# A one-core hybrid block: POOL's phase chain moved behind the last split, and the scaling of the inputs divided between DVE and ACT

## The chip, the cores and the metric

The kernel runs on one core of a Trainium2 chip. The metric is the device time of one execution in microseconds (us), taken as the median of several runs. Engines: PE (matrix multiply) with its weight loads PEld, DVE (elementwise), ACT (activations, copies), POOL (elementwise, and DMA issue), SP (DMA issue). SBUF is the memory on the chip that all of them read; PE writes its results to PSUM, which DVE and ACT read.

## The reference, cut to what matters

One layer of a block: a mixer out of an S5 state-space branch and a gated linear attention (HGRN), then a mixture of experts. The inputs are `x` (1024 tokens of 1024 features) and a context `ctx` (256 tokens), float32. The change concerns how the normalised, modulated inputs are made, and tables of the S5 branch.

```python
mod = jax.nn.silu(c) @ w_ada + b_ada              # shift sh1, scale sc1, ... for the tokens
mod_c = jax.nn.silu(c_ctx) @ w_ada + b_ada        # csh1, csc1, ... for the context
h  = rms_norm(x,   norm1_g) * (1.0 + sc1)  + sh1  # rms_norm: t * rsqrt(mean(t*t) + eps) * g
hc = rms_norm(ctx, norm1_g) * (1.0 + csc1) + csh1
z  = h @ w_in                                     # u (256, for S5), q, ff, fb, i, g_out, gates
zc = hc @ w_in
# S5: powers of exp(lam*dt) per state, products with b_bar and c; the scan over the tokens
```

The root (`rsqrt`) belongs to a token; the factor `norm1_g * (1 + sc1)` and the shift `sh1` belong to a feature.

## The kernel before

x and ctx are held transposed: features on the 128 partitions, 8 tiles k = 0 .. 7 of 128 features, tokens along the columns. There are three streams r: the 256 context tokens (r = 0), tokens 0 to 511 (r = 1), tokens 512 to 1023 (r = 2).

All large products are made in float32 parts: an operand is split into a high part (ACT rounds it to `F32R`) and a low part (DVE subtracts the high part), and `mm3` (lines 81 to 84) does high x high (L82), low x high (L83) and high x low (L84). So a matmul over tile k of a stream waits for ACT's high part `hH` or `hcH` and for DVE's low part.

The front of the kernel is a `manual_schedule` block: in it each engine works in the order in which the lines stand. Its steps:

- `s5_tables` makes tables of the S5 branch on DVE, in short instructions. Then POOL makes `phases(1, G)`: the powers 0 to 159 of a phase for 8 groups, by doubling, 8 rounds of 6 elementwise products and sums (`cmul_steps`, L1233 to L1248), of 8, 16, .. 512 and at last 248 columns, in the buffer `big1`, and two DMAs to `phd` (L1316). Then POOL makes `ca` (two halves of 6 products of 1152 columns), each followed by two DMAs to `cad` (L1328). The same phases for the other direction, `phases(0, V)` in `big0`, are on DVE, handed to the caller as a generator: the caller runs 24 steps of it at once, 3 later and the rest behind the last split. Its two DMAs are issued by POOL as well.
- `stats(r)`: ACT squares the tiles, PE sums them, `rsqrt` (L89 to L93: a root on ACT, a reciprocal and three short instructions on DVE, two of which read two SBUF operands) gives the root per token, and PE spreads it over all partitions into PSUM, `prs[r]` (L279).
- `mods(g)`: PE multiplies a quarter of `w_ada` by the activations of c. Quarters 2 and 3 give the factor `am` early; quarters 0 and 1 give the shift, which `shift` (L317) writes into `mod`.
- `scaled(r, k)` (L284, DVE): x tile times `am` (per partition) times `prs[r]` (PSUM). `split(r, k)`: ACT adds the shift and rounds to the high part (L292); DVE adds the shift again and subtracts the high part (L295).
- The loop over k splits streams 0 and 1, and `z_step` multiplies each tile for the first two 128-column blocks of `w_in` (the u of S5). Four tiles of stream 1 are scaled ahead of the loop and four inside it. Then `scaled(2, k)` and `split(2, k - 1)` run over stream 2, `z_half` does the second half of the tokens, and u goes as `us0`, `us1` to DRAM (`u_out`: `us0` by 8 DMAs of POOL, `us1` by 8 of SP).

Behind the block a planner orders each engine's work. `s5_tables2` makes `wts` on DVE (12 products of 1024 columns), PE transposes them, and matrices `kts` are put together in buffers of the same names `big0` and `big1` and sent to `kd`. `values(0)` multiplies all tokens by the i columns of `w_in`, ten tiles in three PSUM buffers "z", which ACT copies into `vc` (context) and `vt` (L429). Pool "up" with `us0` and `us1` is closed at the end of the block, and pool "vp" with `vt` and `vc` is opened at its place: `vt` begins at the first byte of `us0`, and `vc` lies within `us1`.

Of the kernel before, what the change touches and what calls it, by code (L numbers as in the profile page):

```python
# [10 lines left out]
F32 = mybir.dt.float32  # L11
# [3 lines left out]
AF = mybir.ActivationFunctionType  # L15
ALU = mybir.AluOpType
# [8 lines left out]
P = 128  # L25
D = 1024
KD = D // P
# [16 lines left out]
def tile_kernel(ctx: ExitStack, tc: tile.TileContext, A: dict, dbg=None):  # L44
    nc = tc.nc
    V, S, G, PE = nc.vector, nc.scalar, nc.gpsimd, nc.tensor
# [34 lines left out]
    def mm3(out, lh, ll, rh, rl, start, stop):  # L81
        PE.matmul(out, lh, rh, start=start, stop=False)  # L82
        PE.matmul(out, lh, rl, start=False, stop=False)  # L83
        return PE.matmul(out, ll, rh, start=False, stop=stop)  # L84
# [19 lines left out]
    def half(dt=F32):  # L104

        return hp.tile([P, 512], dt, name="xl", bufs=2 * KD)

    def ctx_row(dt=F32):
        return hcp.tile([P, LC], dt, name="xcl", bufs=KD + 1)
# [32 lines left out]
    am = frp.tile([P, KD, 2], F32, name="am")  # L142
# [9 lines left out]
    def z_half(H, L, n, out=None, ks=range(KD)):  # L152
        ps = zp.tile([P, 512], F32, name="z") if out is None else out
        for k in ks:
            ws = slice(k * P, k * P + P)
            ts = slice(n * 512, n * 512 + 512)
            lastmm[0] = mm3(ps, H[:, ws], L[:, ws], hH[:, k, ts], hL[n][k], k == 0, k == KD - 1)
        return ps
# [8 lines left out]
    with tc.manual_schedule(), tc.tile_pool(name="stp", bufs=1, space=PSUM) as qp, ExitStack() as small:  # L167
        q = small.enter_context(tc.tile_pool(name="st", bufs=1))
# [50 lines left out]
        def am_steps():  # L219
# [6 lines left out]
            )  # L226

        s5t = s5_tables(nc, tc, A, cad, phd, r8d, am_steps, *s5in)
        next(s5t)
        S.activation(lg, lg, AF.Exp)  # L230
# [10 lines left out]
        prs = [qp.tile([P, 512], F32, name=f"prs{r}") for r in range(3)]  # L241
# [38 lines left out]

        def scaled(r, k):
            rows_, _, lo, hi = streams[r]
            c = 1 if r == 0 else 0
            V.scalar_tensor_tensor(  # L284
                rows_[k], rows_[k], am[:, k, c : c + 1], prs[r][:, : hi - lo], ALU.mult, ALU.mult
            )

        def split(r, k):
            rows_, H, lo, hi = streams[r]
            c, ho = (1, 0) if r == 0 else (0, lo)  # L290
            xk, Hk, sh = rows_[k], H[:, k, ho : ho + hi - lo], mod[:, k, c : c + 1]
            S.activation(Hk, xk, AF.Identity, bias=sh)  # L292
            Lk = half(F32R) if r else ctx_row(F32R)
            (hL[r - 1] if r else hcL).append(Lk)
            return V.scalar_tensor_tensor(Lk, xk, sh, Hk.bitcast(F32), ALU.add, ALU.subtract).ins  # L295

        def some(g, n):
            for _ in range(n):
                next(g, None)
# [5 lines left out]
        def u_half(m, n, ps):  # L305
            for c in range(4):

                dst = us[m][:, :, 32:160].rearrange("p j (r c) -> p c j r", c=8)[:, n * 4 + c]
                V.tensor_copy(dst, ps.rearrange("p (c j r) -> p c j r", c=4, j=8)[:, c])

        def u_out(m, E):
            for j in range(8):
                E.dma_start(ud[m].rearrange("(j c) g k -> j g c k", j=8)[j], us[m][:, j])
            dump("us%d" % m, us[m])
# [7 lines left out]
        for g in (2, 3):  # L322
            some(md[g], 3)
        s5mid = next(s5t)
        some(s5mid[3], 24)
        some(st[0], KD + 1)
        some(st[1], 4)
        some(st[0], 1)
# [3 lines left out]
        for k in range(KD - 1):  # L332
            scaled(0, k)
        some(md[0], 1)
        some(st[1], 1)
        scaled(0, KD - 1)
        some(s5mid[3], 3)
        some(st[1], 1)
        some(md[0], 2)
        for k in range(4):  # L340
            scaled(1, k)
        shift(0)
        some(md[1], 2)
        split(0, 0)
        split(1, 0)
        some(md[1], 1)
        H0 = high_w(raws[0])
        L0 = low_w(raws[0], H0)
        split(0, 1)
        split(1, 1)  # L350
        shift(4)
# [7 lines left out]
        def z_step(m, k):  # L359
            H, L = ((H0, L0), (H1, L1))[m]  # L360
            zc_tile(H, L, (pc0, pc1)[m], [k])
            z_half(H, L, 0, (z00, z10)[m], [k])
# [2 lines left out]
        z_step(0, 1)  # L365
        z_step(1, 0)
        for k in range(2, KD):
            if k + 2 < KD:
                scaled(1, k + 2)
            split(0, k)  # L370
            split(1, k)
            some(st[2], PAT[k - 2])
            z_step(0, k)
            z_step(1, k - 1)
# [8 lines left out]
        for k in range(KD + 1):  # L383
            if k < KD:
                scaled(2, k)
            if k in (2, 5):
                u_half(k // 5, 0, (z00, z10)[k // 5])
            if k:
                lastL = split(2, k - 1)
        u_half(0, 1, z_half(H0, L0, 1))  # L390
        u_out(0, G)
        u_half(1, 1, z_half(H1, L1, 1))
# [6 lines left out]


    with tc.issue_after(lastL):
        some(s5mid[3], 99)
    if stop_after <= 1:
        ws_.close(); s5s.close(); early.close(); zs.close(); fr.close()
        return
# [424 lines left out]
    q = xs_.enter_context(tc.tile_pool(name="wo", bufs=1, reuse_waits="tile"))  # L830
# [261 lines left out]
def s5_tables(nc, tc, A, cad, phd, r8d, more, q, qt, par, bt, ct):  # L1092
    V, S, G, PE = nc.vector, nc.scalar, nc.gpsimd, nc.tensor
# [41 lines left out]
    def tsc(a, s1, op0, s2=None, op1=None, o=None):  # L1135
        o = t16() if o is None else o
        if op1 is None:
            E.tensor_scalar(o, a, s1, None, op0)
        else:
            E.tensor_scalar(o, a, s1, s2, op0, op1)  # L1140
        return o
# [11 lines left out]
    r = tsc(n, -PI_HI, ALU.mult)  # L1153
# [71 lines left out]
    def cmul_steps(or_, oi, ar_, ai, br, bi, shp, E=V, own=None):  # L1225

        n_ = int(np.prod(shp))
        t = temp(E, n_, own)
        if len(shp) == 2:
            t = t.rearrange("p (a b) -> p a b", a=shp[0])  # L1230
        if len(shp) == 3:
            t = t.rearrange("p (a b c) -> p a b c", a=shp[0], b=shp[1])
        E.tensor_tensor(or_, ar_, br, ALU.mult)  # L1233
        yield
        E.tensor_tensor(t, ai, bi, ALU.mult)
        yield
        E.tensor_tensor(or_, or_, t, ALU.subtract)
        yield
        E.tensor_tensor(oi, ar_, bi, ALU.mult)
        yield  # L1240
        t2 = temp(E, n_, own)
        if len(shp) == 2:
            t2 = t2.rearrange("p (a b) -> p a b", a=shp[0])
        if len(shp) == 3:
            t2 = t2.rearrange("p (a b c) -> p a b c", a=shp[0], b=shp[1])
        E.tensor_tensor(t2, ai, br, ALU.mult)
        yield
        E.tensor_tensor(oi, oi, t2, ALU.add)  # L1248
        yield

    bb = q.tile([P, 2, 16, 16], F32, name="bb")
# [7 lines left out]
    pw = q.tile([P, 2, 9, 16], F32, name="pw")  # L1259
# [29 lines left out]
    dn = q.tile([P, 2, 9, 16], F32, name="dn")  # L1289
# [8 lines left out]
    ca = q.tile([P, 2, 2, 8, 144], F32, name="ca")  # L1298
    def phases(d, X):

        big = q.tile([P, 2560], F32, name=f"big{d}")
        pt_ = big.rearrange("p (r a k) -> p r a k", r=2, a=8)
        ds_ = slice(d * 8, d * 8 + 8)
        X.memset(pt_[:, 0, :, 0:1], 1.0)
        X.memset(pt_[:, 1, :, 0:1], 0.0)
        X.tensor_copy(pt_[:, 0, :, 1], ph[:, 0, ds_])
        X.tensor_scalar(pt_[:, 1, :, 1], ph[:, 1, ds_], 1.0 - 2.0 * d, None, ALU.mult)
        n_ = 1
        while n_ < 159:
            w_ = min(n_, 159 - n_)  # L1310
            bc = lambda r: pt_[:, r, :, n_ : n_ + 1].broadcast_to([P, 8, w_])
            yield from cmul_steps(pt_[:, 0, :, n_ + 1 : n_ + 1 + w_], pt_[:, 1, :, n_ + 1 : n_ + 1 + w_],
                 pt_[:, 0, :, 1 : 1 + w_], pt_[:, 1, :, 1 : 1 + w_], bc(0), bc(1), (8, w_), E=X)
            n_ *= 2
        for r in range(2):
            G.dma_start(phd[d, r], pt_[:, r])  # L1316

    for _ in phases(1, G):
        pass
    for d in range(2):  # L1320
        ps_ = slice(d * 8, d * 8 + 8)
        pwd = (pw[:, 0], pwn) if d == 0 else (dn[:, 0], dnn)
# [3 lines left out]
        cmul(cv(0), cv(1), c_(0), c_(1), g(0), g(1), (8, 9, 16), E=G)  # L1326
        for r in range(2):
            G.dma_start(cad[d, r], ca[:, d, r])  # L1328
    yield q, qt, cmul, phases(0, V), bb, ca, pw, dn


def s5_tables2(nc, tc, last, lastL, A, ident, kd, wtd, qp, q, qt, cmul, phases, bb, ca, pw, dn):
# [658 lines left out]
```

## Time and profile before

| | |
|---|---|
| median of 3 runs | 2132.8 us (2128.4 to 2133.94) |
| the profiled execution | 2134.74 us |
| its span in the trace | 2133.1 us |
| mean granted clock of PE | 0.976 |
| busy in the span: PE, PEld, DVE, ACT, POOL | 93%, 75%, 61%, 47%, 23% |

The rows below are from the trace of that execution. Times count from the start of the span. A row of the timeline is: start, duration, engine, line of the kernel, operation, what it writes <- what it reads, shape, count; in brackets the idle time of the engine before it and what ended it. POOLq, SPq and ACTq are DMA issues. The granted clock is given as a share of full speed, 1.0 being the upper of PE's two levels (2.4 GHz) and 0.5 the lower (1.2 GHz).

### The profile page before, as it was taken

The page shows a single profiled execution, that of the slowest core. Times are in us where ns is not written, and L with a number is a line of the kernel's source. Part 1 is how long each engine was busy: PE and PEld are TensorE (multiplying, and loading weights), DVE is VectorE, ACT ScalarE, POOL GpSimd, SP SyncE. Part 2 cuts the span into 40 slices and gives each one's busy share as a digit, 9 for nine tenths or more (in the row PEclk, how much of TensorE's full clock was granted, in tenths as well). Part 3 has the DMA queues.
Part 4 walks back from the last instruction along what each step waited for, and adds up shares of the span by engine and source line. Part 5 has one row for each costly group of instructions (what it writes and reads, how often), then busy time and mean ns, then how long its engine had stood idle before and what let it go on. Part 6 is the DMA issues. An engine that isn't in the chain of part 4 may idle for free. (4 is left out here: it accounts for less than half of the span.)

```text
span 2133.1 us, 30727 instructions
## 1 busy us (share of the span) xinstructions
PE 1979.8 (93%) x10313; PEld 1602.0 (75%) x10313; DVE 1295.5 (61%) x2123; ACT 1003.6 (47%) x1418; POOL 485.5 (23%) x399
## 2 busy tenths in 40 slices
PE   6789999999999999997999899899999999999983
PEld 2488889888777788885877688687888887777761
DVE  7864664664577644444558667756655657776736
ACT  4334454544532411112233456756565666766631
POOL 5510000000012000001101234333333334343322
PEclk8799999999999999998999999999999999999997
DMA  8251010101144344438432699888898889998966
GB/s 310 74 142 40 24 46 31 40 31 32 49 143 158 115 134 143 134 104 302 168 131 100 254 297 306 313 266 256 260 302 247 273 261 348 334 314 248 312 159 275
DMA packets 101516, 398.73 MB, mean 187 GB/s; under 512 B 14690, under 2 KB 21474, under 8 KB 79812
## 3 DMA queue, kind: packets, MB, share of 16 engines
q1 hardware_dynamic: 60576, 260.03, 34.3%
q0 software_dynamic: 31168, 117.81, 20.8%
q10 hardware_dynamic: 9572, 18.46, 2.4%
q8 instruction: 98, 1.61, 0.3%
q14 instruction: 102, 0.84, 0.1%
HBM read 456.25 MB, written 81.55 MB: 252 GB/s over the span
## 5 line engine op out<-in xcount | busy, mean ns | idle before, releaser
L1634 DVE TENSOR_TENSOR wl<-raw,wh 128x2048 fp32r<-128x2048 f32 x156 | 352.9, 2290 | 120.2 <-ACT wh L1628 119.1
L1687 PE MATMUL pa<-wh,xh 128*128 128x512 f32 x760 | 305.3, 402 | 0.0
L1688 PE MATMUL pa<-wl,xh 128*128 128x512 f32 x760 | 299.9, 395 | 1.2 <-DVE wl L1634 0.6
L1628 ACT CAST wh<-raw 128x2048 fp32r<-128x2048 f32 x156 | 292.7, 1916 | 0.1
L83 PE MATMUL z<-xl,wH 128*128 128x512 f32 x672 | 270.6, 403 | 8.9 <-DVE xl L295 8.9
L82 PE MATMUL z<-hH,wH 128*128 128x512 f32 x672 | 268.1, 399 | 2.7 <-ACT hH L292 1.6
L84 PE MATMUL z<-hH,wL 128*128 128x512 f32 x672 | 267.0, 397 | 0.0
L1690 PE MATMUL pa<-wh,xl 128*128 128x512 f32 x496 | 193.5, 390 | 0.0
L1687 PE MATMUL py<-wh,hh 128*128 128x512 f32 x380 | 159.0, 418 | 29.4 <-ACT y L1751 19.1
L1757 POOL DMA_INDIRECT acc<-y,si x62 | 98.3, 1586 | 346.3 <-ACT y L1751 206.5
L1688 PEld LDWEIGHTS pa<-wl,xh 128*128 128x128 f32 x760 | 143.5, 189 | 34.5 <-DVE wl L1634 8.0
L1687 PEld LDWEIGHTS pa<-wh,xh 128*128 128x128 f32 x760 | 143.7, 189 | 26.4
L83 PEld LDWEIGHTS z<-xl,wH 128*128 128x128 f32 x672 | 127.4, 190 | 35.6 <-DVE xl L295 12.5
L1688 PE MATMUL py<-wl,hh 128*128 128x512 f32 x380 | 152.8, 402 | 1.2 <-DVE wl L1634 1.2
L1690 PE MATMUL py<-wh,hl 128*128 128x512 f32 x380 | 150.9, 397 | 0.0
L127 DVE TENSOR_TENSOR wL<-wraw,wH 128x1024 fp32r<-128x1024 f32 x56 | 75.0, 1346 | 121.9 <-ACT wH L122 121.8
L82 PEld LDWEIGHTS z<-hH,wH 128*128 128x128 f32 x672 | 127.3, 189 | 27.9 <-ACT hH L292 1.8
L84 PEld LDWEIGHTS z<-hH,wL 128*128 128x128 f32 x672 | 127.6, 190 | 24.5 <-issue 0.7
L1646 POOL DMA_INDIRECT xg<-h2d,gi x63 | 119.7, 1900 | 51.5 <-DVE jk L1677 17.4
L122 ACT CAST wH<-wraw 128x1024 fp32r<-128x1024 f32 x56 | 58.8, 1050 | 148.3 <-PE z L83 65.0
L1718 ACT ACTIVATE sl<-pa 128x256 f32<-128x256 f32 x95 | 36.5, 384 | 191.3 <-DVEq L1715 119.9
L1666 ACT CAST xh<-pt 128x512 fp32r<-128x512 f32 x190 | 102.1, 590 | 35.4 <-PE pt L1656 31.9
(538 smaller groups left out, 4073.9 us busy)
## 6 DMA issues: line engine op xcount, KB each, us to landing
raw<-in_wm_dram SPq DMA_DIRECT2D x285, 1024.0 KB
wraw<-in_wz_dram SPq DMA_DIRECT2D x50, 512.0 KB
wk<-in_w_ada_dram SPq DMA_DIRECT2D x64, 256.0 KB
raw<-in_wm_dram POOLq DMA_DIRECT2D x6, 1024.0 KB, 10.3
acc<-x POOLq DMA_DIRECT2D x9, 512.0 KB, 6.1
xl<-in_xcT_dram SPq DMA_DIRECT2D x16, 256.0 KB
mgd<-ga POOLq DMA_DIRECT2D x16, 256.0 KB, 3.0
xr<-in_xc_dram SPq DMA_DIRECT2D x8, 512.0 KB
```

The source lines that it names most:

```text
L82: PE.matmul(out, lh, rh, start=start, stop=False)
L83: PE.matmul(out, lh, rl, start=False, stop=False)
L84: return PE.matmul(out, ll, rh, start=False, stop=stop)
L127: V.tensor_tensor(L, raw, H.bitcast(F32), ALU.subtract)
L1628: S.copy(WH[b, c], raw[b % 2][c])
L1634: V.tensor_tensor(WL[b, c], raw[b % 2][c], WH[b, c].bitcast(F32), ALU.subtract)
L1646: G.indirect_dma_start(XG[b], None, h2d, IndirectOffsetOnAxis(ap=gi[:, b : b + 1], axis=0))
L1666: S.copy(xh[:, s], PX[b][hf])
L1687: PE.matmul(out, lh, rh, start=start, stop=False)
L1688: PE.matmul(out, lh, rl, start=False, stop=stop and ll is None)
L1690: PE.matmul(out, ll, rh, start=False, stop=stop)
L1757: G.indirect_dma_start(accs[b % 2], IndirectOffsetOnAxis(ap=si[:, b : b + 1], axis=0), y, None, compute_op=ALU.add)
```

## The change

- `scaled` multiplies by the root alone (DVE, one operand in PSUM), for all streams. The factor `am` goes into `split`: ACT multiplies by it and adds the shift, in place, and a second ACT instruction copies the result to the high part; DVE subtracts the high part from it.
- All eight tiles of stream 1 are scaled ahead of the loop.
- `phases(1, G)` is no longer run inside `s5_tables`. It is handed to the caller, which runs it behind the last `split(2, 7)` and ahead of `u_out(0, G)`. Its first instruction, once a memset of ones, copies a column `gate`, which DVE sets to 1.0 behind the last split.

```diff
         def scaled(r, k):
             rows_, _, lo, hi = streams[r]
-            c = 1 if r == 0 else 0
-            V.scalar_tensor_tensor(
-                rows_[k], rows_[k], am[:, k, c : c + 1], prs[r][:, : hi - lo], ALU.mult, ALU.mult
-            )
+            V.tensor_tensor(rows_[k], rows_[k], prs[r][:, : hi - lo], ALU.mult)
 
         def split(r, k):
             rows_, H, lo, hi = streams[r]
             c, ho = (1, 0) if r == 0 else (0, lo)
             xk, Hk, sh = rows_[k], H[:, k, ho : ho + hi - lo], mod[:, k, c : c + 1]
-            S.activation(Hk, xk, AF.Identity, bias=sh)
+            S.activation(xk, xk, AF.Identity, bias=sh, scale=am[:, k, c : c + 1])
+            S.copy(Hk, xk)
             Lk = half(F32R) if r else ctx_row(F32R)
             (hL[r - 1] if r else hcL).append(Lk)
-            return V.scalar_tensor_tensor(Lk, xk, sh, Hk.bitcast(F32), ALU.add, ALU.subtract).ins
+            return V.tensor_tensor(Lk, xk, Hk.bitcast(F32), ALU.subtract).ins
...
-        some(s5mid[3], 24)
+        some(s5mid[3][0], 24)
...
-        some(s5mid[3], 3)
+        some(s5mid[3][0], 3)
         some(st[1], 1)
         some(md[0], 2)
-        for k in range(4):
+        for k in range(KD):
             scaled(1, k)
...
         for k in range(2, KD):
-            if k + 2 < KD:
-                scaled(1, k + 2)
             split(0, k)
             split(1, k)
...
                 lastL = split(2, k - 1)
+
+        V.memset(s5mid[3][2], 1.0)
+        some(s5mid[3][1], 99)
         u_half(0, 1, z_half(H0, L0, 1))
         u_out(0, G)
         u_half(1, 1, z_half(H1, L1, 1))
...
     with tc.issue_after(lastL):
-        some(s5mid[3], 99)
+        some(s5mid[3][0], 99)
...
-        X.memset(pt_[:, 0, :, 0:1], 1.0)
+        if d:
+            X.tensor_copy(pt_[:, 0, :, 0:1], gate.unsqueeze(1).broadcast_to([P, 8, 1]))
+        else:
+            X.memset(pt_[:, 0, :, 0:1], 1.0)
...
-    for _ in phases(1, G):
-        pass
+    gate = q.tile([P, 1], F32, name="gate")
     for d in range(2):
...
-    yield q, qt, cmul, phases(0, V), bb, ca, pw, dn
+    yield q, qt, cmul, (phases(0, V), phases(1, G), gate), bb, ca, pw, dn
```

## Rows read from the trace of the kernel before

**Rows 1.** The page, part 1: busy time, share of the span, instructions.
```profile
PE 1979.8 (93%) x10313; PEld 1602.0 (75%) x10313; DVE 1295.5 (61%) x2123; ACT 1003.6 (47%) x1418; POOL 485.5 (23%) x399
```

**Rows 2.** Busy time per stretch: the stretch, its length, engines, clock, DMA share.
```profile
51.70:97.00 45.30, 31.90 (x122) 19.96 (x123) 37.28 (x26) 14.64 (x28) 32.79 (x16) 0.74 0.27 102
51.70:68.00 16.30, 9.43 (x24) 5.02 (x24) 16.30 (x9) 5.81 (x10) 16.13 (x9) 0.50 0.30 109
85.80:97.00 11.20, 11.20 (x57) 8.06 (x56) 3.19 (x9) 2.86 (x7) 0.00 (x0) 0.85 0.19 72
111.20:144.20 33.00, 28.80 (x289) 26.96 (x288) 27.76 (x48) 10.72 (x20) 5.98 (x10) 0.95 0.58 175
144.20:200.00 55.80, 54.68 (x340) 48.19 (x339) 14.58 (x25) 21.44 (x36) 1.92 (x4) 1.00 0.21 49
```

**Rows 3.** PE's waits, 30 to 111 us: total, times, longest.
```profile
PE z L83 <- DVE xl L295: 8.9, 7, 2.3
```

**Rows 4.** The timeline of POOL in the first 120 us.
```profile
23.46 0.48 POOL L1306 COPY big<-ph 128x8 f32<-128x8 f32 x1 [21.05 <-DVE ph L1237]
...
37.67 1.05 POOL L1233 TENSOR_TENSOR big<-big 128x512 f32<-128x512 f32 x1
...
48.88 1.20 POOL L1316 DMA_DIRECT2D phd<-big  x2
50.09 2.26 POOL L1233 TENSOR_TENSOR ca<-ct,pw 128x1152 f32<-128x1152 f32 x1
...
58.12 2.43 POOL L1239 TENSOR_TENSOR ca<-ct,pwn 128x1152 f32<-128x1152 f32 x1
...
83.70 1.13 POOL L1328 DMA_DIRECT2D cad<-ca  x2
113.94 4.82 POOL L313 DMA_DIRECT2D ud<-us  x8 [29.11 <-DVE big L1248]
```

**Rows 5.** The timeline of DVE in the first 112 us.
```profile
25.87 0.18 DVE L1233 TENSOR_TENSOR big<-big 128x8 f32<-128x8 f32 x1
...
30.27 0.15 DVE L90 RECIPROCAL rs_y<-rs_y 128x2 f32<-128x2 f32 x1
...
37.76 0.97 DVE L93 SCALAR_TENSOR_TENSOR rs_y<-rs_t,rs_y 128x4 f32<-128x4 f32 x1
...
45.78 0.17 DVE L317 TENSOR_TENSOR mod<-pm,b 128x8 f32<-128x8 f32 x1 [1.71 <-PE pm L255]
...
58.37 2.73 DVE L295 SCALAR_TENSOR_TENSOR xl<-xl,mod,hH 128x512 fp32r<-128x512 f32 x1
...
64.21 0.73 DVE L284 SCALAR_TENSOR_TENSOR xl<-xl,am,prs 128x512 f32<-128x512 f32 x1
...
85.29 0.74 DVE L295 SCALAR_TENSOR_TENSOR xl<-xl,mod,hH 128x512 fp32r<-128x512 f32 x1
...
109.61 1.62 DVE L295 SCALAR_TENSOR_TENSOR xl<-xl,mod,hH 128x512 fp32r<-128x512 f32 x2
```

**Rows 6.** The timeline of PE: the first z matmul.
```profile
51.75 0.56 PE L82 MATMUL prs<-hcH,wH 128*128 128x256 f32 x1
```

**Rows 7.** The timeline of ACT: a split, a copy into vc, the third into vt.
```profile
46.40 0.71 ACT L292 ACTIVATE hH<-xl,mod 128x512 fp32r<-128x512 f32 x1
...
128.25 0.37 ACT L429 COPY vc<-z 128x256 f32<-128x256 f32 x1 [6.26 <-DMA wraw<-in_wz_dram]
...
143.73 0.37 ACT L429 COPY vt<-z 128x256 f32<-128x256 f32 x1 [3.41 <-PE z L84]
```

**Rows 8.** Instructions on the tile us: duration min/median/max in ns, first to last.
```profile
L313 SPq DMA_DIRECT2D ud<-us x8: 570/572/1597, 118.8 to 124.4; - x8
...
DMA to landing us min/median/max: 2.4/2.6/2.7
```

**Rows 9.** DVE's groups, 111.2 to 144.2 us: busy us, mean ns.
```profile
L1248 DVE TENSOR_TENSOR wts<-wts,cmt 128x1024 f32<-128x1024 f32 x2 | 2.5, 1226 | 0.1
...
L309 DVE COPY us<-z 128x128 f32<-128x128 f32 x8 | 2.3, 413 | 0.2 <-PE z L84 0.2
```

## The prediction

> **What bounds the kernel now.** I read the page's busy shares first: PE is busy for 93% of the span [rows 1], so time is to be had only where PE stands still. The table by stretches and PE's list of waits say where near the change: between 51.7 and 97.0 us PE works 31.9 of 45.3 us at a mean granted clock of 0.74 [rows 2], and its largest wait there is for DVE's subtractions (L295), 8.9 us in 7 waits [rows 3]. The rows of POOL and DVE side by side show why. A subtraction that starts at 58.37, while POOL runs a product from 58.12 to 60.55, takes 2.73 us; the same form takes 0.74 us at 85.29, when POOL is done [rows 4, 5]. An instruction on four columns takes 0.97 us at 37.76 because POOL works from 37.67 to 38.72. L284, whose second tensor lies in PSUM, takes its 0.73 us at 64.21 beside a busy POOL. So **a DVE instruction with two SBUF inputs waits for the end of POOL's instruction**, however short it is itself; with one SBUF input it doesn't. From 144 us on PE is dense (54.7 of 55.8 us) [rows 2]: what is lost or won before stays in the time.
>
> **The change, part by part.** The profiled execution took 2134.7 us (span 2133.1), 1.9 above the median of the runs, 2132.8; I sum against it and take the 1.9 off at the end.
>
> **1. POOL's queue in front.** Before, the chain of phases (48 products of 8 to 512 columns) goes from 23.46 to 48.88, and after its two DMA issues the 12 products of `ca`, 1152 columns each, from 50.09 to 83.70, in two halves with a DMA issue of 1.1 us behind each [rows 4]. Taking the phases away doesn't free POOL in front: the `ca` products move up, since they need only `pw` and its negatives, which DVE has done just before its own phases start at 25.87 [rows 5]. They last 33.6 us, less some 3 of waiting for DVE's long instructions, so from about 25 to 57. What DVE has queued there is another thing than at 50 to 84: first 24 steps of its own phases (8 to 64 columns, two SBUF inputs each; before, 25.87 to 30.27 us, beside POOL's equally short ones), and behind them the roots of the streams, of which each has two such instructions, and on which the scaling of x, PE's broadcast and the modulation wait. Each of these short instructions now waits for a product, 2.26 us for the first of the twelve [rows 4]. At the 12 ends of products one slips in, sometimes two; while POOL issues the first DMAs (1.1 us) some eight do. That is about 20 of 24 by the time that `ca` ends: the first root starts at 57.7 instead of 30.27 [rows 5], **27.4 us late**. (Were two to slip in at each end, it would be 52, 22 late.)
>
> **2. From the root to the first matmul.** Before, 30.27 to 45.78 for the shift, 15.5 us [rows 5], and 6.0 more to the first z matmul at 51.75 [rows 6]. POOL is now silent: about 1.5 us of lock waits go (0.97 instead of 0.16 is one). PE comes cold out of a long pause, some 1.0 of half-rate work; four more scalings stand in DVE's queue before the shift, 4 x 0.66 = 2.6 us, but beside PE's modulation, 0.4 late. So 15.4 + 6.0: first z matmul at 79.1.
>
> **3. The split loop.** PE's work in it is 31.9 us x 0.74 = 23.6 at the full clock [rows 2]; with the start at the lower clock, as the last stretch lost 15% of 11.2 us, 25.3. DVE has two subtractions per step, under 0.74 us each. ACT gets a second instruction per split. A copy of 512 columns from SBUF is in no row here; below it lies nothing, above it the activation with scale and bias that it follows, 0.71 us at 46.40 [rows 7]; I take 0.55, and 0.3 for the 256 columns. Per step 0.5 + 0.3 + 0.71 + 0.55 = 2.1 us, with two squares 3.2, and PE's step is 25.3 / 8 = 3.2: level, and both hidden by each other; at 0.71 per copy it costs 1 us over the loop. The loop ends at 104.4 instead of 97.0: **+7.4 us, of 27.4 late 20 are given back.** If PE's clock stays at 0.50, as it did from 51.7 to 68 [rows 2], the loop takes over 40 us.
>
> The Trainium skill speaks against part 1 (SBUF — State Buffer, Summary: rules for kernel authors): of a two-input DVE instruction and a reading GpSimd instruction the second to issue is fully blocked, so whichever is off the critical path should be scheduled elsewhere. Used on the split loop alone, that rule gives its 20 us; used on the whole of POOL's queue it forbids 12 long products over 24 short steps. The rows agree with it in both places.
>
> **4. The last stage** (97 to 111.2, the second half of the tokens): before, scaling and subtraction of 0.66 each per k on DVE; now DVE the same within 0.1, ACT 0.71 + 0.55 per k. ACT's 1.3 and DVE's 1.3 are level; 0 to 2, I take 0. The last split ends at 118.6 instead of 111.2 [rows 5].
>
> **5. Behind the last split.** Here POOL's queue decides. Before, `u_out(0, G)` issues at 113.94, for 4.82 us, and lands 2.6 later [rows 4, 8]. Now the 48 phases, two `phd` DMAs and only then these eight stand in the queue. `us0` lies where `vt` will lie: pool "up" is closed and "vp" opens at the same place of the stack, and `vt` begins at `us0`'s first byte. The trace shows this wait already, for `us1` and `vc`: SP issues the last of `us1` at 124.4, it lands 2.6 us later, and ACT's first copy into `vc` goes at 128.25 after 6.26 us of idleness, though PE had long ended that tile [rows 7, 8]. So ACT's first copy into `vt` waits for POOL. z has three PSUM buffers: PE can do the tile for `vt` copies one to three, which it has at 143.73 before [rows 7], and then stops.
>
> How long do the phases take? At least the 25.4 us they took before. At most that plus DVE's two-input work in this stretch: 27.8 us busy from 111.2 to 144.2 [rows 2], less 2.3 of copies from PSUM [rows 9], so 25.4 + 25.5 = 51. By turns of one and one, with DVE sometimes waiting for PE, I take three quarters: 25.4 + 19 = 44, nearer to the upper row since both queues are full. In the times of before (add 7.4): start 111.3, phases to 155.3, `phd` 1.2, `ud` 4.8, landing 2.6, so `vt` is free at 163.9. PE stands from 143.7: 20 us, less 3 of transposes of `wts` that need no z buffer: **+17 us** (0 at the lower end, 26 at the upper). PE is dense behind it, so nothing of it is won back. The two `phd` issues of DVE's own phases stand behind in the same queue; where ACT's order puts the copies into their buffer ahead of `vt`, another 5.
>
> Sum: 2134.7 + 7.4 + 0 + 17 = 2159.1; less 1.9, **2157 us**.
>
> **Rivals.** (a) *Only the front counts.* POOL's phases run at their old 25.4 us, since DVE gives way; `vt` is free at 145 and PE hardly stops. 2132.8 + 7.4 = 2140. For it: small POOL and DVE instructions got by each other from 25.9 to 30.3 at little cost. Against: then both were under 0.4 us, here DVE's are 1.23 us each for `wts` [rows 9].
> (b) *Faster.* DVE's 24 short steps slip between the products of `ca` and the chain stays at its old times; the loop starts at 51.7 and takes 25 to 28 instead of 45: -17. With the tail of (a) about 2116; it decides where the first root starts before 40 us. Against it: the four columns at 37.76 that waited 0.8 us for POOL.
> (c) *Both ends cancel*: the front of (b), the tail of my forecast: 2133.
> (d) *Worse.* The loop stays at the lower clock (+16), or ACT's queue also stands behind the late `phd` DMAs (+5) with phases at 51 us (+9): 2171 to 2178.
>
> **How the numbers follow.** My forecast 0.54 (2143 to 2170 by its own bounds), (a) 0.16, (b) 0.09, (c) 0.07, (d) 0.14. The range leaves out most of (b) and the end of (d): 2133 to 2174. A change under 0.3% (6.4 us) can't be told from none in this kernel. Faster takes (b) and a part of (c): 0.11. Same takes the rest of (c) and those of (a) below 2139: 0.12. Slower: 0.77.
>
> **What would show it.** Right: `ca` products on POOL from about 25; DVE's phase steps one per product, 2 us and longer each; the first RECIPROCAL (L90) after 50; z matmuls from 75 to 80 with no L295 of 2 us or more; the `ud` issues on POOL behind the phases, after 140; a gap of 10 us or more on PE before the third or fourth `vt` copy. Wrong: a first root before 40; phases of 27 us behind the last split; `vt` copies at a steady 2.9 us.

## The result, and the profile after

The changed kernel took **2163.6 us** (median of 3 runs, 2159.59 to 2164.47) against 2132.8: a ratio of 1.014 [1.0124, 1.0155], 30.8 us slower. The forecast was 2157, 24 slower, by two losses: 7.4 us in front of the last split and 17 behind it. The first was nearly right. The second was there, and larger, but another wait than the one forecast set it.

The page of the changed kernel, part 1 (answers to [rows 1]): PE has the same 10313 instructions, 5.6 us more busy time, 29.7 us more span.

```profile
PE 1985.4 (92%) x10313; PEld 1607.1 (74%) x10313; DVE 1296.1 (60%) x2124; ACT 1018.0 (47%) x1442; POOL 492.6 (23%) x399
```

POOL's timeline (columns as in [rows 4]: start, duration). The `ca` products now begin at 25.62 instead of 50.09. The phases run from 119.26, behind the gate, to 151.62, and the eight DMAs of `ud` go out behind them.

```profile
25.62 2.37 POOL L1232 TENSOR_TENSOR ca<-ct,pw 128x1152 f32<-128x1152 f32 x1 [23.39 <-DVE pw L1236]
...
57.12 1.13 POOL L1329 DMA_DIRECT2D cad<-ca  x2
119.26 0.19 POOL L1304 COPY big<-gate 128x8 f32<-128x8 f32 x1 [61.01 <-DVE gate L387]
...
151.62 1.17 POOL L1318 DMA_DIRECT2D phd<-big  x2
152.78 4.24 POOL L311 DMA_DIRECT2D ud<-us  x7
157.73 0.60 POOL L311 DMA_DIRECT2D ud<-us  x1 [0.72 <-DMA phd<-big]
159.48 1.16 POOL L1318 DMA_DIRECT2D phd<-big  x2 [1.16 <-DMA ud<-us]
```

DVE's timeline (answers to [rows 5]):

```profile
29.69 0.16 DVE L1308 COPY big<-ph 128x8 f32<-128x8 f32 x1
...
29.75 2.23 DVE L1309 TENSOR_SCALAR big<-ph 128x8 f32<-128x8 f32 x1
...
34.73 2.18 DVE L1245 TENSOR_TENSOR cmt<-big 128x8 f32<-128x8 f32 x1
36.95 2.17 DVE L1247 TENSOR_TENSOR big<-big,cmt 128x8 f32<-128x8 f32 x1
...
42.31 5.11 DVE L1234 TENSOR_TENSOR cmt<-big 128x32 f32<-128x32 f32 x1
...
57.97 0.16 DVE L90 RECIPROCAL rs_y<-rs_y 128x2 f32<-128x2 f32 x1
...
72.78 0.15 DVE L315 TENSOR_TENSOR mod<-pm,b 128x8 f32<-128x8 f32 x1
...
118.47 0.69 DVE L293 TENSOR_TENSOR xl<-xl,hH 128x512 fp32r<-128x512 f32 x1 [0.67 <-ACT hH L290]
...
139.05 1.54 DVE L1234 TENSOR_TENSOR cmt<-dn,bb 128x1024 f32<-128x1024 f32 x1
158.74 0.21 DVE L1372 TENSOR_TENSOR big<-big,pk 16x64 f32<-16x64 f32 x1 [18.16 <-ACT big L1371]
158.88 1.21 DVE L1236 TENSOR_TENSOR wts<-wts,cmt 128x1024 f32<-128x1024 f32 x1
```

Products of 8 columns, 0.18 us before, can take 2.2 us beside POOL's products of 1152 columns: of the 24 early steps 9 waited like this. The first root comes at 57.97 instead of 30.27. The last split ends at 118.47 + 0.69 = 119.16 instead of 111.23. And at 158.74 DVE has stood for 18.16 us at a small addition whose input an ACT copy makes. ACT's timeline says what that copy waited for:

```profile
88.41 0.81 ACT L289 ACTIVATE xl<-xl,mod,am 128x512 f32<-128x512 f32 x1
89.25 0.62 ACT L290 CAST hH<-xl 128x512 fp32r<-128x512 f32 x1
...
157.55 0.57 ACT L1370 COPY big<-pk 16x512 f32<-16x512 f32 x1 [30.29 <-DMA phd<-big]
158.13 0.52 ACT L1371 COPY big<-pk 16x448 f32<-16x448 f32 x1
...
162.63 0.66 ACT L428 COPY vc<-z 128x256 f32<-128x256 f32 x2
163.16 0.41 ACT L428 COPY vt<-z 128x256 f32<-128x256 f32 x1
```

ACT stood for 30.29 us ahead of its copy of `kts` into `big1`: that buffer holds POOL's phases until their DMAs have read it. (The rows leave buffer numbers out. When this copy started, at 157.55, only the `phd` DMAs of POOL's phases, at 151.62, had been issued; those of `big0` went at 159.48.) `wts`, which PE transposes, stands in DVE's queue behind the blocked addition, and so PE stands too.

PE's own timeline has the first z matmul at 76.89 (51.75 in [rows 6]), the broadcast of stream 2's root, where the loop ends, and the end of the stop:

```profile
76.89 0.56 PE L82 MATMUL prs<-hcH,wH 128*128 128x256 f32 x1
...
103.61 1.36 PE L279 MATMUL prs<-dg,ones 128*128 128x128 f32 x8
...
160.15 1.97 PE L1349 MATMUL pt<-ident,wts 128*128 128x128 f32 x8 [22.60 <-DVE wts L1236]
```

By stretch (columns as in [rows 2]: the stretch, its length, busy us of PE, PEld, DVE, ACT, POOL, granted clock):

```profile
77.00:104.40 27.40, 26.88 (x127) 18.83 (x126) 11.71 (x22) 23.47 (x45) 0.00 (x0) 0.88 0.18 58
119.20:152.00 32.80, 18.34 (x206) 16.10 (x204) 20.22 (x34) 2.10 (x2) 31.49 (x53) 0.84 0.21 67
```

The split loop is as dense as forecast (26.88 of 27.40 us, where it was 31.90 of 45.30 before). Behind the last split PE works 18.34 of 32.80 us.

### The profile page after: what moved, and what is told of

Read it like the earlier page. It is cut to its first block, busy times and chain, and to the rows that moved or that the text cites. A ratio compares the mean times of both kernels' runs of the same rounds, so it can differ in the third digit from the quotient of the medians.

```text
span 2162.8 us, 30759 instructions
## 1 busy us (share of the span) xinstructions
PE 1985.4 (92%) x10313; PEld 1607.1 (74%) x10313; DVE 1296.1 (60%) x2124; ACT 1018.0 (47%) x1442; POOL 492.6 (23%) x399
## 5 line engine op out<-in xcount | busy, mean ns | idle before, releaser
L127 DVE TENSOR_TENSOR wL<-wraw,wH 128x1024 fp32r<-128x1024 f32 x56 | 68.5, 1231 | 125.5 <-ACT wH L122 125.3
L1667 ACT CAST xh<-pt 128x512 fp32r<-128x512 f32 x190 | 102.1, 591 | 30.8 <-PE pt L1657 27.5
```

Source lines behind the costliest of these rows:

```text
L127: V.tensor_tensor(L, raw, H.bitcast(F32), ALU.subtract)
L1667: S.copy(xh[:, s], PX[b][hf])
```

## The experiments

All kernels compute the whole reference. They are read by three marks of the trace: the first root (L90), the end of the last split, and ACT's first copy into `qt`, behind which the medians differ from before by 4 us or less (experiment 10 by 6: its profiled execution took 2135.1 us, its median is 2141.2). Each mark is read from one execution. The fourth column is the time from the split's end to that copy, less the 53.3 us of before (111.2 to 164.46): what was lost (+) or won (-) behind the split. The ratio is against the kernel before on the same chip, so it tells differences of a few us better than the medians, and where two experiments ran on different chips, their ratios are compared.

| kernel | first root | last split | behind it | ratio to before |
|---|---|---|---|---|
| before | 30.27 | 111.2 | 0 | 1 |
| after | 57.97 | 119.2 | +22.1 | 1.014 [1.0124, 1.0155] |
| 1: POOL's move alone | 55.40 | 111.8 | +21.4 | 1.0115 [1.0082, 1.0148] |
| 2: new scaling alone | 30.62 | 114.1 | -1.9 | 1.0009 [0.9991, 1.0027] |
| 3: after, `ud` first | 55.54 | 117.9 | +23.8 | 1.0156 [1.0126, 1.0185] |
| 4: after, DVE's steps late | 27.52 | 95.2 | +17.8 | 1.0026 [1.0009, 1.0043] |
| 5: `ca`, then phases; steps late | 30.44 | 95.8 | -3.3 | 0.9916 [0.9894, 0.9937] |
| 6: 4, unbound behind | 27.43 | 95.7 | +3.2 | 0.9932 [0.9914, 0.995] |
| 7: 6, old scaling | 29.07 | 93.8 | +2.3 | 0.9932 [0.9913, 0.995] |
| 8: after, unbound behind | 55.67 | 118.1 | -2.1 | 1.0029 [1.0018, 1.0039] |
| 9: `ca` late; steps late | 25.79 | 84.3 | +26.6 | 1.0007 [0.9994, 1.0019] |
| 10: `ca`, then phases alone | 55.33 | 113.4 | -0.1 | 1.0028 [1.0018, 1.0037] |
| 11: steps late alone | 27.39 | 106.3 | -4.4 | 0.9937 [0.9924, 0.995] |
| 12: 5, new scaling | 28.82 | 97.0 | -2.7 | 0.9915 [0.99, 0.993] |

### The two parts by themselves (1 and 2)

Experiment 1 is before with only the move of POOL's phases (the diff's last hunks, its gate and its call); experiment 2 is before with only the new `scaled`, `split` and loop.

> Only POOL's phases are moved; scaling and split stay as before the change. Theory (POOL's queue carries the whole loss): first root near 58 us again, last split near 118 to 121, PE idle 20 to 24 us behind it; 2158 to 2166 us. Rival (the second ACT instruction per split costs the time): about 2135 to 2145.

> Only the scaling and split are changed; POOL's phases stay in front. Theory: DVE still makes two subtractions per step under the products of ca, so the loop is as long as before, ACT's second instruction is hidden: last split at 109 to 114, 2130 to 2137 us. Rival (the divided split shortens the loop of itself, by 10 us or more): 2115 to 2125.

The move of POOL's queue alone gives 2155.8, 25 us above before on the same chip (2130.8), with the late root (55.40) and the stop behind the split, for `wts` as after:

```profile
PE pt L1353 <- DVE wts L1240: 24.1, 1, 24.1
```

It missed its expectation in front: the last split, expected at 118 to 121, ends at 111.8, and so the time is below 2158. The new scaling alone gives 2133.4: no difference that is clear of noise. Its loop is not shorter (45.4 us against 45.2), though DVE's instruction is simpler, as long as POOL's products stand beside it. Put on top of the moved queue the new scaling costs 5 us by the ratios (1.0140 against 1.0115), but their intervals overlap. The marks show it more plainly: 7.4 us at the last split (119.2 against 111.8), or 6.1 and 6.3 by experiments 3 and 8, whose front is that of after.

### Which wait stops PE (3, 6, 8)

Experiment 3 is after with the two lines exchanged, so that `us0` is free early:

```diff
         V.memset(s5mid[3][2], 1.0)
-        some(s5mid[3][1], 99)
         u_half(0, 1, z_half(H0, L0, 1))
         u_out(0, G)
+        some(s5mid[3][1], 99)
```

> The changed kernel with us0's eight DMAs ahead of the phases in POOL's queue. Rival, as the prediction had it (vt's copies wait for these DMAs): the gap on PE goes to under 8 us, 2145 to 2150 us. Theory now (ACT's first waiting copy is that into big1, behind the phd DMAs of the phases): the gap stays, and the phases start later behind the DMAs, so 2162 to 2168 us.

The forecast's wait is gone: ACT's first copy into `vt` goes at 138.58. The stop is not. PE's transposes now wait for ACT's copy of the ones before them, which stands behind the copy of `kts`; ACT's timeline, and PE's waits from 100 to 240 us:

```profile
138.58 0.39 ACT L428 COPY vt<-z 128x256 f32<-128x256 f32 x1
168.89 0.57 ACT L1370 COPY big<-pk 16x512 f32<-16x512 f32 x1 [29.92 <-DMA phd<-big]
```
```profile
PE pt L1349 <- ACT wt L1350: 26.0, 2, 25.7
```

So the theory "`vt` behind `ud`" falls as the cause, and "`kts` behind `phd`" holds: the `phd` DMAs go 10 us later (162.02), and the copy into `big` 11 us later. The proof is to take this wait away. Experiment 8 keeps the changed kernel's front and frees both: `ud` first as above, and

```diff
-            G.dma_start(phd[d, r], pt_[:, r])
+            (G if d else nc.sync).dma_start(phd[d, r], pt_[:, r])
...
-            kts = q.tile([P, 2560], F32, name=f"big{b8}")[:16, :1920].rearrange("c (g t) -> c g t", g=8)
+            kts = q.tile([P, 2560], F32, name="big0")[:16, :1920].rearrange("c (g t) -> c g t", g=8)
```

so that `kts` no longer uses POOL's buffer, and the other direction's DMAs don't stand in POOL's queue.

> The changed kernel with the unbinding of e6 alone; DVE's 24 steps stay in front. Theory: last split at 117 to 119 as in the changed kernel, no long gap behind it: 2139 to 2146 us, the 7 to 8 us of the front left over. Rival (the gap is DVE's own lateness): 2152 us or more.

2138.9: of the 30.8 us, 24 to 25 are gone (by the ratios and by the medians), though POOL's phases end still later (at 168.0). PE's longest wait from 118 to 200 us is now

```profile
PE pkt L544 <- DVE sgc L496: 0.9, 1, 0.9
```

Experiment 6 makes the same edits and also the one of experiment 4:

> As e4, and nothing that ACT copies waits for POOL's phases any more: us0's DMAs go ahead of them, both kts are built in big0, and SP issues the phd DMAs of DVE's phases. POOL's phases still run behind the last split, beside DVE. Theory (the gap is ACT's queue waiting for the phd and ud DMAs): the gap of 21 us shrinks to under 6, 2114 to 2122 us. Rival (DVE, slowed by POOL's instructions, is late with wts by itself): a gap of 10 us or more is left, 2126 us or more.

By the ratios it takes 20 us off experiment 4 (0.9932 against 1.0026). So the cost behind the split is shown from both sides: 20 to 25 us, and it goes with the `kts` buffer and the two queues, not with POOL's time. Of the three edits, experiment 3 shows that `ud` first does nothing alone; the buffer and SP's issues weren't tried apart, and in 8 the planner also puts `vc` and the first `vt` ahead of `kts` in ACT's order, as it did in 3.

### DVE's steps under POOL's products (4, 11, 10, 5)

Experiment 4 is after, experiment 11 is before, without the two lines that run 27 steps of DVE's own phases early (all then run behind the last split):

```diff
         s5mid = next(s5t)
-        some(s5mid[3], 24)
...
         scaled(0, KD - 1)
-        some(s5mid[3], 3)
```

> The changed kernel without DVE's 27 steps of its own phases in front; they run behind the last split. Theory (12 long products over 24 short steps make the late root): two roots with two waiting instructions each, first root before 36 us, first z matmul near 60, last split near 101, the gap behind it as in the changed kernel plus some 3 us: 2143 to 2150 us. Rival (the modulation's weights or POOL's products themselves set the start): last split still after 112, 2158 us or more.

> The kernel before with DVE's 27 steps behind the last split as the only edit; POOL's order as before. Theory: the root comes 3 us earlier, the loop still runs under the products of ca until 80 or so: last split at 107 to 111, 2128 to 2134 us. Rival (DVE's early steps alone cost what e5 won): 2115 to 2122.

In 4 the root comes at 27.52 with `ca` on POOL beside it, 30.5 us earlier than after: what delayed it was what DVE had queued ahead of it, as the forecast said. The time, 2136.9, is below the 2143 to 2150 expected, since the last split comes at 95.2 and not near 101.

```profile
27.52 0.16 DVE L90 RECIPROCAL rs_y<-rs_y 128x2 f32<-128x2 f32 x1
```

The last split ends 24 us earlier than after and 16 earlier than before, and behind it 17.8 more are spent than before, so that the 16 are lost again: with `ud` late as well, the wait for `phd` stands at the same place, and PE's stop ends at ACT's `vc` copies behind it.

```profile
131.92 0.58 ACT L1368 COPY big<-pk 16x512 f32<-16x512 f32 x1 [28.69 <-DMA phd<-big]
...
136.51 0.37 ACT L426 COPY vt<-z 128x256 f32<-128x256 f32 x1 [1.36 <-DMA ud<-us]
```
```profile
PE z L82 <- ACT vc L426: 21.3, 1, 21.3
```

(The second line of the first fence is the forecast's wait: 1.36 us.) Experiment 11 missed its expectation: 2120.8, 13 us under before on the same chip (2133.7), with POOL's work unchanged. 4.9 us of it are there at the last split: the shift is ready at 41.81 instead of 45.78. 4.4 come behind (the rest lies behind the mark and wasn't followed), and they are the same chain as in the changed kernel from ACT's queue on, small. In the kernel before, ACT stood for 6.26 us ahead of its copy into `vc` at 128.25 [rows 7]. Right behind it in ACT's timeline, and then in DVE's:

```profile
128.65 0.58 ACT L1369 COPY big<-pk 16x512 f32<-16x512 f32 x1
129.24 0.53 ACT L1370 COPY big<-pk 16x448 f32<-16x448 f32 x1
```
```profile
129.80 0.22 DVE L1371 TENSOR_TENSOR big<-big,pk 16x64 f32<-16x64 f32 x1 [3.52 <-ACT big L1370]
```

and PE's longest wait of before from 95 to 240 us (in experiment 11 the transposes wait 1.1 us for `wts`):

```profile
PE pt L1348 <- DVE wts L1237: 4.2, 1, 4.2
```

There the copy into `vc` stood ahead of the `kts` copy in ACT's order; in experiment 11 the planner has the `kts` copies ahead, at 115.93 and 118.38:

```profile
115.93 0.58 ACT L1367 COPY big<-pk 16x512 f32<-16x512 f32 x1 [2.41 <-PE pk L1364]
...
118.38 0.58 ACT L1367 COPY big<-pk 16x512 f32<-16x512 f32 x1 [1.34 <-DVE big L1369]
...
122.04 0.65 ACT L427 COPY vc<-z 128x256 f32<-128x256 f32 x2 [2.53 <-DMA ud<-us]
```

That the order of these copies makes the 4.4 us is read from the two traces; it wasn't tried by itself.

Experiment 10 is before with POOL's two jobs exchanged, phases ungated behind `ca`; experiment 5 does that and removes DVE's early steps:

```diff
-    for _ in phases(1, G):
-        pass
     for d in range(2):
...
             G.dma_start(cad[d, r], ca[:, d, r])
+    for _ in phases(1, G):
+        pass
```

> The kernel before with POOL's order alone swapped: ca first, phases right behind; DVE's 24 steps stay in front. Theory (the short DVE steps under long products are the loss in front): first root at 55 to 58, last split at 112 to 120, no gap behind: 2134 to 2143 us. Rival (POOL's order is worth the gain of e5 by itself): 2115 to 2122.

> The kernel before, with two orders changed in front: POOL makes ca first and its phases right behind, without a gate, and DVE's 27 steps of its phases run behind the last split. Theory: root near 27, loop from about 50 beside POOL instructions of at most 1.3 us, last split at 95 to 100; nothing of POOL is late behind it, so no gap: 2115 to 2122 us. Rival (DVE's 27 steps behind the split take as much there): 2130 or more.

| ratio to before | DVE's steps early | DVE's steps late |
|---|---|---|
| phases, then `ca` | 1 | 0.9937 |
| `ca`, then phases | 1.0028 | 0.9916 |

With the steps early the exchange makes the root late (55.33) and loses 0.28%, though the loop is shorter. With the steps late it brings the last split 10.5 us forward, but the ratios show only 0.2% (some 4 us) of gain, and their intervals overlap; where the rest goes isn't shown. Neither edit's worth can be told from the other's alone. **Experiment 5 is the best version run, 0.9916 of before** (experiment 12 equals it), without the gate and without the new scaling. Its loop and that of experiment 11, from the first z matmul to the broadcast of stream 2's root (experiment 11 first):

```profile
46.70:92.00 45.30, 31.35 (x122) 19.64 (x122) 40.29 (x26) 15.23 (x29) 37.61 (x21) 0.77 0.30 116
```
```profile
50.50:81.00 30.50, 26.22 (x123) 17.86 (x123) 21.88 (x26) 15.41 (x29) 29.40 (x49) 0.83 0.27 93
```

DVE's 26 instructions take 40.29 us beside the products of `ca`, and 21.88 beside the phases, with POOL busy for 83% and 96% of the two stretches (in experiment 5 `ca` ends at 59.1). So for this loop it is not that POOL works, but how long each of its instructions is.

### The new scaling once nothing else binds (7 and 12), and `ca` behind (9)

Experiment 7 is 6 with the old `scaled` and `split`; experiment 12 is 5 with the new ones.

> e6 with scaling and split as before the change (one ACT instruction per split). Theory: ACT's second instruction sets the step of the loop when no product is in the way (3.35 us against PE's 3.1), so this is 2 to 5 us faster than e6: 2111 to 2119 us. Rival (ACT's part is hidden): the same as e6 within 1 us.

> e5 with the changed scaling and split. Theory (ACT's second instruction sets the loop's step once DVE is free): 2 to 6 us slower than e5, 2118 to 2124 us. Rival (hidden): equal to e5 within 1 us.

Both ratios are equal to their partner's within 0.0001 (0.9932 and 0.9932, 0.9915 and 0.9916). ACT's doubled work costs 1.2 to 1.9 us at the last split (95.7 against 93.8; 97.0 against 95.8). Nothing of it is to be seen in the time, where the intervals of about 0.2% either way would hide some 4 us.

Experiment 9 is before with the phases in front as they were, DVE's steps late, and the `ca` products issued behind `u_out(0, G)`:

```diff
         u_out(0, G)
+        s5mid[3][1]()
...
-    for d in range(2):
+    def late_ca():
+        for d in range(2):
...
```

> The kernel before, with ca (not the phases) behind us0's DMAs in POOL's queue and DVE's 27 phase steps late. Theory: no long POOL product in front and none over the loop; first root near 27, loop of 25 us, last split at 86 to 92. Behind it ca takes 32 to 45 us and kts wait for it; if ACT's queue has vt's copies ahead of kts, 2105 to 2115 us; if ACT's queue stops at kts again, with a gap of 10 us or more on PE, 2118 to 2130.

Both theories missed it. The front is the best of all (last split at 84.3, loop 25.4 us), and all 27 us go back behind it: PE's waits, 95 to 240 us,

```profile
PE pt L1348 <- DVE wts L1236: 14.3, 2, 14.1
PE pk L1366 <- POOL ca L1236: 10.7, 2, 6.5
```

PE needs `ca` itself there, and DVE's phases, now beside products of 2.3 us, make `wts` late. POOL's queue adds to it: the last product of `ca` stands behind a `phd` DMA that waits for DVE's phases.

```profile
129.32 0.59 POOL L1315 DMA_DIRECT2D phd<-big  x1 [8.54 <-DVE big L1236]
```

So of POOL's two jobs `ca` is the one that can't go behind the last split as it stands here; the phases can, once their buffer holds nobody up (experiments 6 and 8), and they fit beside the loop (experiment 5).

## Why the prediction was right or wrong

**1, POOL's queue in front: right in its mechanism, and luck in its last digits.** First root forecast at 57.7, measured at 57.97, by the mechanism named: short steps that wait for a product, 2.2 us each. But the terms erred both ways. The steps began at 31.89 (before, 25.87): an earlier product of DVE's had waited for POOL too (2.24 us at 25.78), and so had the TENSOR_SCALAR at 29.75. Ten products stood over the steps, not twelve; none to two steps got by at the end of one, and four beside the first DMA issues where eight were guessed; 20 of the 24 were through when `ca` ended, as forecast. And in this execution all of it is 2.4 us late by something else, a wait of DVE for PE's modulation ahead of `ca`: in experiments 3 and 8, with the same front, `ca` begins at 23.18 and the root comes at 55.54 and 55.67. From the start of `ca` to the root it is 32.4 or 32.5 us in all three. Experiment 4 confirms the cause.

One sentence of the part before it was too broad, that an instruction with one SBUF input doesn't wait: the TENSOR_SCALAR of eight columns at 29.75 took 2.23 us (the copy ahead of it 0.16). Also, the 8.9 us in 7 waits quoted there are those from 30 to 111 us; from 51.7 to 97.0 PE waits 6.0 us in 3 for these subtractions, still its largest wait. The rule of the Trainium skill cited there (SBUF — State Buffer, Summary: rules for kernel authors) agrees with the 9 two-input steps that waited; experiments 4 and 5 follow it, by taking the short work away from the long products, and have the first root at 27.52 and 30.44.

**2, to the first matmul: 2 us too long.** Shift forecast 15.4 us behind the root, measured 14.8; from there 6.0 more forecast, 4.1 measured; the matmul forecast at 79.1, measured at 76.89. The four more scalings ahead of the shift were priced at 0.4 us and cost 1.2: PE ended the modulation at 71.58, and the shift starts behind the scalings at 72.78.

**3, the loop: right in kind, 1.4 us short.** Forecast 25.3 us to the broadcast, measured 26.7 (76.89 to 103.61). ACT's price was mis-sized: activation and copy of 512 columns 0.81 + 0.62, of 256 columns 0.59 + 0.40, 2.42 against 2.1 by the forecast. Its 0.71 us "with scale and bias" was misread: the activation at 46.40 has a bias alone. With 1.1 of squares that makes a step of 3.5 us, longer than PE's 3.2, and ACT is busy for 9.94 of the loop's first 10.10 us; behind them, with fewer squares, for 13.26 of 16.60, and there PE sets the pace. With one ACT instruction per split (experiment 1) the loop takes 25.0 us, with two (experiments 3 and 8) 26.1 and 26.0. The end came at 103.61 for 104.4, since step 2 had erred the other way.

**4, the last stage: 0 forecast, and 1.2 us measured** (119.16 less 103.61 is 15.55; before, 111.23 less 96.91, where that broadcast stood, is 14.32; experiments 6 and 7 differ by the same 1.2 there, so it is ACT's second instruction). Last split: +7.4 forecast, +7.9 measured. Experiment 8 gives this half its price in the whole: 6.1 us.

**5, behind the last split: this step failed in its cause and its terms, not in its sign.** Three things:

- The duration. POOL's phases were to take 44 us by three quarters of DVE's work in the way; they took 32.4. DVE had 20.2 us of work there instead of 27.8, and from 140.6 none: it stood behind the blocked addition itself, so that the last third of POOL's chain ran undisturbed. The collision was priced as if DVE's queue stayed full. (The upper end of the term was added up wrongly too: 51 us of phases make 27 us of standing, less 3, so 24 and not 26.)
- The waiter. The forecast's `vt` behind `ud` exists (1.36 us in experiment 4), and freeing it changes nothing (experiment 3). The wait that counts stands earlier in ACT's queue, and starts from the `phd` DMAs, not from `ud`. It was named only as an extra of 5 us in step 5 and rival (d). The sign given for this step, a gap on PE before the third or fourth `vt` copy, wasn't met either: the stop came before the first of them, at 163.16. The kernel before showed the chain in its rows: PE's 4.2 us for `wts`, behind DVE's 3.52 for ACT's copy, quoted above. I had read PE's wait as DVE being busy and didn't follow it through the head of DVE's queue.
- The price. PE stopped from 137.55 (160.15 less 22.60) to 160.15, in the times of before 129.6 to 152.2, against a forecast of 143.7 to 163.9: 14 us earlier and 12 earlier. Two errors of opposite sign leave a stop of 22.6 us for 20; by the mark at `qt`, +22.1 for +17. That is most of the distance from 2157 to 2163.6. In this half it was luck that the number came near: the chain, the start of the stop and its end were all others than forecast.

**The rivals.** (a), only the front counts, 2140: what experiment 8 gives, 2138.9, once the buffers are apart; in the kernel as it stands it is out. (b) is out by the root at 57.97, yet its idea is right one edit further: without the early steps the last split ends 16 us before its old time, and experiment 6, with the tail freed too, gives 2119 for the rival's 2116. (c) is nearly what experiment 4 is: front and tail cancel, 2136.9 for its 2133. (d) has the right waiter and the wrong companions: the loop's clock rose to 1.00, and the phases were short.

## What to carry to other kernels

Work that is moved off a crowded stretch must be followed through every buffer that it holds: look up who next writes that memory, find that instruction in its engine's queue, and list what stands behind it there, and behind those in their queues; a wait at the head of three queues in turn (ACT's copy, DVE's addition, PE's transposes) cost 22 us here, the late front 8. And before a long POOL product is moved, read what the other engine has queued beside it: short DVE instructions can lose one long product each (9 of 24 did here), so put short beside short. Two small edits, DVE's early steps left out and POOL's two jobs exchanged, gave 0.8% where the larger change lost 1.4%.

## What the runs showed of the hardware that was not expected

- DVE instructions slip by POOL's in bursts: of 24 short steps beside products of 2.3 us 15 waited for none (about half of these beside POOL's DMA issues), 8 for one, and one of 32 columns for two (5.11 us at 42.31, with POOL's DMA issue at its beginning).
- A long pause of PE isn't the same for the clock each time. After, PE waited 26.1 us for the root, and from 76.9 to 87.0 the granted clock was 0.67, then 1.00. In experiment 10 it waited 29.0 us, and the whole loop was at 1.00. What PE did between pause and loop differed little (12.90 of 18.90 us busy, 13.86 of 17.60). In between lie experiments 3, 8 and 1, with waits of 28 to 29 us and 0.73, 0.81 and 0.83 in the first 10 us of the loop. The cause stays open. The stretches, of after and of experiment 10:

```profile
58.00:76.90 18.90, 12.90 (x73) 6.54 (x73) 10.83 (x32) 8.41 (x18) 0.25 (x1) 0.77 0.63 231
76.90:87.00 10.10, 9.65 (x35) 6.66 (x35) 6.53 (x10) 9.94 (x18) 0.00 (x0) 0.67 0.31 104
87.00:103.60 16.60, 16.53 (x87) 11.64 (x87) 5.29 (x13) 13.26 (x27) 0.00 (x0) 1.00 0.10 33
```
```profile
55.30:72.90 17.60, 13.86 (x72) 7.52 (x72) 12.10 (x28) 7.24 (x16) 16.58 (x45) 0.68 0.58 215
72.90:83.00 10.10, 7.43 (x36) 4.74 (x35) 10.10 (x11) 8.38 (x15) 9.87 (x10) 1.00 0.44 162
```
